# Half of the MLP weights' lower parts formed by an adding DMA instead of VectorE

## The chip, the cores and the metric

The kernel runs on one core of a Trainium2 chip. A core has five engines with queues of their own: TensorE (PE, matmuls; its weight loads are shown as PEld), VectorE (DVE), ScalarE (ACT), GpSimd (POOL) and SyncE (SP, which here only issues transfers). Sixteen DMA engines carry out the transfers that SP, ACT and POOL issue. SBUF is the on-chip memory with 128 partitions, PSUM holds the matmuls' sums.

The metric is the time of one execution in microseconds. The kernel before took 1623.62 us (median of two runs, 1623.09 to 1624.16).

## The reference

One layer of a decoder with 256 tokens behind 16 meta tokens and a width of 2048: a mixer (forgetting attention beside gated linear attention), then an MLP with squared ReLU and 8192 hidden channels. All is float32. What matters for the change is the MLP:

```python
def squared_relu_mlp(xn, w1, w2):
    return jnp.square(jax.nn.relu(xn @ w1)) @ w2

def reference(x, meta_tokens, ...):
    ...
    for l in range(DEPTH):
        h = h + hybrid_mixer(rmsnorm(h, norm_mix_g[l]), w_in[l], ...)
        h = h + squared_relu_mlp(rmsnorm(h, norm_mlp_g[l]), w_ff1[l], w_ff2[l])
    return rmsnorm(h, final_norm_g)[:, N_META:]
```

## The kernel before

**Numbers in two parts.** PE multiplies in a format (`F32R`) with fewer bits than float32. So every operand is split: an upper part `hi`, which is the value rounded to that format, and a lower part `lo`, which is the value less `hi`. A product of two split operands is made of three: `hi` times the upper and lower parts of the activations, and `lo` times their upper part. In `mac2` the first two are one matmul over 512 columns (line 136) and the third is one over 256 (line 137); both go to one PSUM bank `ps`.

**Weights in blocks.** The host lays all weights out as one array `w_all` of blocks of 2048 rows by 128 columns, in the order in which they are used (`stream`). A block is 128 partitions by 16 pieces (`KT`) of 128 columns, 1 MiB. It is fetched and split in two halves of eight pieces (`HK`), 512 KB each, by `weight_half`, whose `step` is:

```python
nc.sync.dma_start(raw[:, cols], w_all[c][:, i * HK * P + cols.start : i * HK * P + cols.stop])
r = raw.rearrange("p (k m) -> p k m", m=P)[:, k, :]
nc.scalar.copy(hi[:, k, :], r)
nc.vector.tensor_tensor(lo[:, k, :], r, hi[:, k, :].bitcast(F32), op=ALU.subtract)
```

So SP issues the load of `raw` (line 118), ACT rounds it to `whi` (line 120, a cast), and DVE subtracts to get `wlo` (line 121). `raw`, `whi` and `wlo` have five buffers each, for five halves, two and a half blocks. `next_weights` calls this for both halves of the next block; `gemm2` runs the 16 pairs of matmuls of a block.

**The MLP.** It goes through the hidden channels in four groups (`NG`). Each group has 16 blocks of the first matrix (ff1, lines 824 to 831), each followed by `relu2`, which evicts `ps`, applies the squared ReLU and splits the result to `a`; and then 16 blocks of the second matrix (ff2, lines 833 to 839), each followed by `add_residual`, which adds `ps` to the residual stream `ht`. In the last group the last four ff2 blocks (`NL`) are made in another way, with the upper parts of their weights kept (lines 842 to 875), since the final norm and the output are overlapped with them. In that group `square_sum` also adds up the squares for the final norm, on POOL (line 768). The output projection ahead of the MLP (lines 791 to 796) does the same for the MLP's norm.

**What sets the order.** The program is written block after block. A scheduler with a model of the times then sets the order of instructions on each engine, so that loads and splits run ahead of the matmuls as far as the buffers allow. Each engine works through its queue in order, and waits on semaphores for what it needs from others. A transfer issued by POOL stands in POOL's queue, with what POOL computes.

Of the kernel before, what the change touches and what calls it, by code (L numbers as in the profile page):

```python
# [7 lines left out]
F32 = mybir.dt.float32  # L8
# [3 lines left out]
AF = mybir.ActivationFunctionType  # L12
ALU = mybir.AluOpType
# [3 lines left out]
P = 128  # L17
# [48 lines left out]
def trunk(ctx: ExitStack, tc: tile.TileContext, hT, w_small, w_all, consts, w_alpha2, out):  # L66
    nc = tc.nc
    serial = [0]

    def nm(s):  # L70
        serial[0] += 1
        return f"{s}_{serial[0]}"
# [11 lines left out]
    def bank(pool, s):  # L84
        return pool.tile([P, 512], F32, tag="bank", name=nm(s))
# [7 lines left out]
    def issued():  # L93
        for e in list(waiting):
            e[0] -= 1
            if e[0] <= 0:
                waiting.remove(e)
                e[1]()
# [6 lines left out]
    chunk = [0]  # L105
    HK = KT // 2

    def weight_half(c, i, hi=None):

        raw = wp.tile([P, HK * P], F32, tag="raw", name=nm("raw"), bufs=RAW)  # L110
        if hi is None:
            hi = wp.tile([P, HK, P], F32R, tag="whi", name=nm("whi"))
        lo = wp.tile([P, HK, P], F32R, tag="wlo", name=nm("wlo"))

        def step(k0, n):
            k = slice(k0, k0 + n)
            cols = slice(k0 * P, (k0 + n) * P)
            nc.sync.dma_start(raw[:, cols], w_all[c][:, i * HK * P + cols.start : i * HK * P + cols.stop])
            r = raw.rearrange("p (k m) -> p k m", m=P)[:, k, :]
            nc.scalar.copy(hi[:, k, :], r)  # L120
            nc.vector.tensor_tensor(lo[:, k, :], r, hi[:, k, :].bitcast(F32), op=ALU.subtract)  # L121

        return hi, lo, step

    def next_weights(keep_hi=None):
        c = chunk[0]
        chunk[0] += 1
        parts = []
        for i in range(2):
            hi, lo, step = weight_half(c, i, None if keep_hi is None else keep_hi[:, HK * i : HK * (i + 1), :])  # L130
            step(0, HK)
            parts.append((hi, lo))
        return lambda k: (parts[k // HK][0][:, k % HK, :], parts[k // HK][1][:, k % HK, :])

    def mac2(ps, hi, lo, x, first, last):
        nc.tensor.matmul(ps, hi, x, start=first, stop=False)  # L136
        nc.tensor.matmul(ps[:, 0:NT], lo, x[:, 0, :], start=False, stop=last)  # L137

    def gemm2(w, x, k0=0, nk=KT):

        ps = bank(pg, "ps")
        for k in range(nk):
            hi, lo = w(k0 + k)
            mac2(ps, hi, lo, x[:, k], k == 0, k == nk - 1)
        issued()
        return ps

    def gemm_all(w, x, n=NA):

        ps = bank(pg, "psa")  # L150
        for k in range(KT):
            hi, lo = w(k)
            nc.tensor.matmul(ps[:, 0:n], hi, x[:, k, 0, :], start=(k == 0), stop=False)  # L153
            nc.tensor.matmul(ps[:, 0:n], lo, x[:, k, 0, :], start=False, stop=False)  # L154
            nc.tensor.matmul(ps[:, 0:n], hi, x[:, k, 1, :], start=False, stop=(k == KT - 1))  # L155
        issued()
        return ps
# [63 lines left out]
    def operand(pool, name, per_k, per_half, at=0, tag=None):  # L221


        kw = {} if tag is None else {"tag": tag}
        t = pool.tile([P, KT, per_k], F32R, name=nm(name), **kw)
        return t[:, :, at : at + per_half + NT].rearrange("p k (o t) -> p k o t", t=NT) if per_half == NT else \
            t[:, :, at : at + 2 * per_half].rearrange("p k (o t) -> p k o t", t=per_half)[:, :, :, 0:NT]
# [25 lines left out]
    def gain(i, k):  # L253
        return h[:, k, NA + i : NA + i + 1]
# [57 lines left out]
    for s in range(KT // 2):  # L312
# [5 lines left out]
        for kk in range(2):  # L318
            k = 2 * s + kk
# [41 lines left out]
    for i in range(2):  # L361
        hi = wp.tile([P, HK, P], F32R, tag="whi", name=nm("whi"))
        lo = wp.tile([P, HK, P], F32R, tag="wlo", name=nm("wlo"))
# [73 lines left out]
    def gla_gates(ts):  # L437
        sg = att.tile([P, 4, NT], F32, tag="sg", name=nm("sg"))
        for i in range(4):
            t = ts[i] if ts else total(gemm2(next_weights(), x[:, :, :, NM:NA]))  # L440
            nc.vector.tensor_tensor(t, t, rbt, op=ALU.mult)
            nc.scalar.activation(sg[:, i, :], t, AF.Sigmoid)
            nc.vector.tensor_tensor(sg[:, i, :], sg[:, i, :], t, op=ALU.mult)
        return sg
# [13 lines left out]
    def gla_head(hd, sg, ready=None):  # L458
# [4 lines left out]
        for i in range(2):  # L463
            ps = ready[1] if ready and i == 0 else gemm_all(next_weights(), x)
            nc.vector.tensor_tensor(ki[:, i, :], ps[:, 0:NA], rb, op=ALU.mult)
        for i in range(2):
            t = qd[:, i, :] if ready else total(gemm2(next_weights(), x[:, :, :, NM:NA]))
            nc.vector.scalar_tensor_tensor(qd[:, i, :], t, GLA_DK ** -0.5, rbt, op0=ALU.mult, op1=ALU.mult)
# [140 lines left out]
    ps = gemm_all(lambda k: (small[k // HK][0][:, k % HK, :], small[k // HK][1][:, k % HK, :]), x)  # L609
# [150 lines left out]
    x2 = operand(keep, "x2", 528, NT, tag="s2")  # L760

    def square_sum(j, acc):
        if j == 0:
            nc.scalar.activation(acc, ht[:, j, :], AF.Square)
        else:
            sq = gat.tile([P, NT], F32, tag="hsq", name=nm("hsq"))
            nc.scalar.activation(sq, ht[:, j, :], AF.Square)  # L767
            nc.gpsimd.tensor_tensor(acc, acc, sq, op=ALU.add)  # L768

    def add_residual(j, ps):  # L770
        b = tmp.tile([P, NT], F32, tag="evb", name=nm("evb"))
        nc.scalar.copy(b, ps[:, NT:512])
        nc.vector.tensor_tensor(ht[:, j, :], ps[:, 0:NT], ht[:, j, :], op=ALU.add)
        nc.vector.tensor_tensor(ht[:, j, :], ht[:, j, :], b, op=ALU.add)
# [38 lines left out]
    def relu2(a, f, ps):  # L813
        t = total(ps)
        nc.vector.scalar_tensor_tensor(t, t, 0.0, r2b, op0=ALU.max, op1=ALU.mult)
        s = gat.tile([P, NT], F32, tag="asq", name=nm("asq"))
        nc.vector.tensor_tensor(s, t, t, op=ALU.mult)
        split_to(a[:, f, 0, :], a[:, f, 1, :], s)

    acc = gat.tile([P, NT], F32, tag="acc", name="acc3", bufs=1)  # L820
    for g in range(NG):
        a = operand(keep, "a", 544, 272, tag="s1")
        held = []
        for f in range(KT):
            ps = gemm2(next_weights(), x2)
            if g == 0 and f == 0:
                held.append(ps)
                continue
            if g == 0 and f == 1:
                relu2(a, 0, held.pop())  # L830
            relu2(a, f, ps)
        last = g == NG - 1
        for j in range(KT - NL if last else KT):
            add_residual(j, gemm2(next_weights(), a))
            if last:
                square_sum(j, acc)
                nc.scalar.activation(ht[:, j, :], ht[:, j, :], AF.Identity, scale=gain(2, j))
                if j == 0:
                    tc.keep_in_program_order(nc.scalar.preload_act_table_set("sqrt_and_others"))
# [4 lines left out]
    for n in range(NL):  # L844
        j, ps = KT - NL + n, bank(pg if n < 3 else px, "ps")
# [49 lines left out]
    v, p, none = nc.vector, nc.gpsimd, lambda: None  # L895
# [81 lines left out]
```

## Time and profile before

| | |
|---|---|
| median of the runs | 1623.62 us |
| the profiled execution's own time | 1623.76 us |
| its span on the chip (first to last instruction) | 1621.7 us |
| granted TensorE clock, mean | 0.997 |
| DMA packets, data moved | 90841, 292.96 MB |
| mean rate | 181 GB/s |

How to read the profile: it shows one execution. An engine's busy time is the time in which it ran instructions, and for PE this is not PE at its peak, since matmuls are pipelined. A line number such as L121 is that of the code line that made the instruction. The chain of waits is followed back from the last instruction, at each step to what released it, or to the instruction before it on its engine. The DMA share is the mean share of the time in which the 16 DMA engines had a packet in work; it can pass 1, where packets overlap. "To landing" is from a transfer's issue to its completion. q1 is the queue of SP's transfers, q0 that of POOL's (software_dynamic).

The MLP fills the span from about 900 us on. In its steady part the rows of the 40 equal slices of the span read 9 of 10 for PE in all of them, and 5 of 10 for the DMA engines.

### The profile page before, as it was taken

The page shows a single profiled execution, that of the slowest core. Times are in us where ns is not written, and L with a number is a line of the kernel's source. Part 1 is how long each engine was busy: PE and PEld are TensorE (multiplying, and loading weights), DVE is VectorE, ACT ScalarE, POOL GpSimd, SP SyncE. Part 2 cuts the span into 40 slices and gives each one's busy share as a digit, 9 for nine tenths or more (in the row PEclk, how much of TensorE's full clock was granted, in tenths as well). Part 3 has the DMA queues.
Part 4 walks back from the last instruction along what each step waited for, and adds up shares of the span by engine and source line. Part 5 has one row for each costly group of instructions (what it writes and reads, how often), then busy time and mean ns, then how long its engine had stood idle before and what let it go on. Part 6 is the DMA issues. An engine that isn't in the chain of part 4 may idle for free.

```text
span 1621.7 us, 25628 instructions
## 1 busy us (share of the span) xinstructions
PE 1609.0 (99%) x10000; PEld 1447.0 (89%) x10000; DVE 1030.6 (64%) x1589; ACT 787.8 (49%) x1212; POOL 92.8 (6%) x144
## 2 busy tenths in 40 slices
PE   9999999999999999999999999999999999999997
PEld 8999999999998888888888888888888888888887
DVE  7866747476555555555677766567655676567654
ACT  6655444454445444444555444444444444444553
POOL 1000000010000000000011000000000000000022
PEclk9999999999999999999999999999999999999998
DMA  9444445454445555555555555555565555555552
GB/s 315 149 142 159 163 158 170 155 197 158 156 157 174 189 186 191 185 191 185 190 188 192 183 189 188 190 187 189 181 195 188 190 187 189 188 189 188 187 180 89
DMA packets 90841, 292.96 MB, mean 181 GB/s; under 512 B 9160, under 2 KB 21712, under 8 KB 90592
## 3 DMA queue, kind: packets, MB, share of 16 engines
q1 hardware_dynamic: 89472, 289.69, 55.1%
q8 instruction: 78, 1.28, 0.3%
q0 software_dynamic: 176, 1.12, 0.2%
q10 hardware_dynamic: 1072, 0.52, 0.1%
q14 instruction: 43, 0.35, 0.1%
HBM read 289.19 MB, written 2.11 MB: 180 GB/s over the span
## 4 chain that ended last, share of the span: by engine, by line
PE 99%; DMA 0%; ACT 0%; DVE 0%; SPq 0%; issue 0%; DVEq 0%; ACTq 0%
PE ps L136 51%; PE ps L137 26%; PE psa L155 5%; PE psa L154 5%; PE psa L153 5%; PE ps L334 1%; PE ps L864 1%; PE ps L339 1%; PE pa L504 1%; PE ps L848 0%; DMA h<-hT_dram 0%; PE po L568 0%; PE pz L402 0%; PE po L569 0%; PE pq L665 0%; PE po L182 0%
## 5 line engine op out<-in xcount | busy, mean ns | idle before, releaser
L121 DVE TENSOR_TENSOR wlo<-raw,whi 128x1024 fp32r<-128x1024 f32 x522 | 639.7, 1225 | 497.4 <-ACT whi L120 496.1
L120 ACT CAST whi<-raw 128x1024 fp32r<-128x1024 f32 x522 | 548.3, 1050 | 744.1 <-PE ps L136 502.0
L136 PE MATMUL ps<-x,whi 128*128 128x512 f32 x1952 | 685.8, 394 | 0.0
L137 PE MATMUL ps<-x,wlo 128*128 128x256 f32 x1952 | 548.0, 281 | 0.0
L136 PEld LDWEIGHTS ps<-x,whi 128*128 128x128 f32 x1952 | 366.4, 188 | 83.2
L137 PEld LDWEIGHTS ps<-x,wlo 128*128 128x128 f32 x1952 | 367.1, 188 | 0.0
L136 PE MATMUL ps<-a,whi 128*128 128x512 f32 x960 | 335.8, 394 | 0.0
L137 PE MATMUL ps<-a,wlo 128*128 128x256 f32 x960 | 269.7, 282 | 0.0
L136 PEld LDWEIGHTS ps<-a,whi 128*128 128x128 f32 x960 | 180.1, 188 | 41.0
L153 PE MATMUL psa<-x,whi 128*128 128x272 f32 x640 | 186.3, 291 | 0.0
L155 PE MATMUL psa<-x,whi 128*128 128x272 f32 x640 | 186.0, 291 | 0.0
L154 PE MATMUL psa<-x,wlo 128*128 128x272 f32 x640 | 184.5, 288 | 0.0
L137 PEld LDWEIGHTS ps<-a,wlo 128*128 128x128 f32 x960 | 181.4, 189 | 0.4
L153 PEld LDWEIGHTS psa<-x,whi 128*128 128x128 f32 x640 | 121.1, 189 | 0.7
L154 PEld LDWEIGHTS psa<-x,wlo 128*128 128x128 f32 x640 | 120.4, 188 | 0.2
L155 PEld LDWEIGHTS psa<-x,whi 128*128 128x128 f32 x640 | 120.2, 188 | 0.1
L136 PE MATMUL ps<-og,whi 128*128 128x512 f32 x256 | 89.9, 393 | 0.0
L136 PE MATMUL ps<-y,whi 128*128 128x512 f32 x256 | 89.1, 392 | 0.0
L768 POOL TENSOR_TENSOR acc<-acc,hsq 128x256 f32<-128x256 f32 x26 | 28.8, 1110 | 774.4 <-ACT hsq L767 774.4
L137 PE MATMUL ps<-y,wlo 128*128 128x256 f32 x256 | 71.8, 281 | 0.0
L137 PE MATMUL ps<-og,wlo 128*128 128x256 f32 x256 | 71.7, 280 | 0.0
L165 DVE TENSOR_TENSOR evt<-ps,evb 128x256 f32<-128x256 f32 x158 | 65.8, 417 | 0.2 <-ACT evb L162 0.2
(263 smaller groups left out, 1384.7 us busy)
## 6 DMA issues: line engine op xcount, KB each, us to landing
raw<-w_all_dram SPq DMA_DIRECT2D x537, 512.0 KB, 4.0
raw<-w_all_dram SPq DMA_DIRECT2D x7, 384.0 KB, 6.0
h<-hT_dram SPq DMA_DIRECT2D x7, 275.0 KB, 6.1
out_dram<-h SPq DMA_DIRECT2D x5, 256.0 KB, 2.6
negc<-fdram POOLq DMA_DIRECT2D x1, 1088.0 KB, 6.1
raw<-w_all_dram SPq DMA_DIRECT2D x2, 256.0 KB, 3.7
raw<-w_all_dram SPq DMA_DIRECT2D x2, 192.0 KB, 3.8
room<-w_small_dram SPq DMA_DIRECT2D x1, 320.0 KB, 6.9
```

The lines of the kernel that those rows point to most:

```text
L120: nc.scalar.copy(hi[:, k, :], r)
L121: nc.vector.tensor_tensor(lo[:, k, :], r, hi[:, k, :].bitcast(F32), op=ALU.subtract)
L136: nc.tensor.matmul(ps, hi, x, start=first, stop=False)
L137: nc.tensor.matmul(ps[:, 0:NT], lo, x[:, 0, :], start=False, stop=last)
L153: nc.tensor.matmul(ps[:, 0:n], hi, x[:, k, 0, :], start=(k == 0), stop=False)
L154: nc.tensor.matmul(ps[:, 0:n], lo, x[:, k, 0, :], start=False, stop=False)
L155: nc.tensor.matmul(ps[:, 0:n], hi, x[:, k, 1, :], start=False, stop=(k == KT - 1))
L165: nc.vector.tensor_tensor(t, ps[:, 0:NT], b, op=ALU.add)
L334: nc.tensor.matmul(ps, hi, x[:, k, :, NM:NA], start=st, stop=False)
L339: nc.tensor.matmul(ps[:, 0:NT], lo, x[:, k, 0, NM:NA], start=False, stop=sp)
L504: nc.tensor.matmul(dst, k[:, a, :], q[:, a, :], start=(a == 0), stop=(a == 1))
L768: nc.gpsimd.tensor_tensor(acc, acc, sq, op=ALU.add)
```

## The change

`weight_half` has a new argument, `by_dma`. Where it is set, DVE makes no subtraction. ACT writes the negated upper part into the lower part's buffer (line 123 of the new file), and POOL issues a transfer that reads the same 512 KB of weights from memory once more and adds them onto that buffer (line 124). `next_weights` sets it for the second half (`i == 1`) of a block only, and the MLP's two calls of `gemm2` ask for it. This holds for the 64 ff1 blocks and for 60 of the 64 ff2 blocks; the last four ff2 blocks, and all blocks ahead of the MLP, are split as before. Of these lines, the numbers shift by seven: the matmuls of `mac2` are lines 143 and 144 in the new file.

```diff
-    def weight_half(c, i, hi=None):
+    def weight_half(c, i, hi=None, by_dma=False):
...
             nc.scalar.copy(hi[:, k, :], r)
-            nc.vector.tensor_tensor(lo[:, k, :], r, hi[:, k, :].bitcast(F32), op=ALU.subtract)
+            if by_dma:
+                nc.scalar.activation(lo[:, k, :], hi[:, k, :].bitcast(F32), AF.Copy, scale=-1.0)
+                nc.gpsimd.dma_start(lo[:, k, :].rearrange("p k m -> p (k m)"),
+                                    w_all[c][:, i * HK * P + cols.start : i * HK * P + cols.stop], accum_op=ALU.add)
+            else:
+                nc.vector.tensor_tensor(lo[:, k, :], r, hi[:, k, :].bitcast(F32), op=ALU.subtract)
...
-    def next_weights(keep_hi=None):
+    def next_weights(keep_hi=None, by_dma=False):
...
-            hi, lo, step = weight_half(c, i, None if keep_hi is None else keep_hi[:, HK * i : HK * (i + 1), :])
+            hi, lo, step = weight_half(c, i, None if keep_hi is None else keep_hi[:, HK * i : HK * (i + 1), :],
+                                       by_dma and i == 1)
...
-            ps = gemm2(next_weights(), x2)
+            ps = gemm2(next_weights(by_dma=True), x2)
...
-            add_residual(j, gemm2(next_weights(), a))
+            add_residual(j, gemm2(next_weights(by_dma=True), a))
```

In the orders of instructions that the prediction quotes, `whi`, `wlo` and `raw` are the three tiles of a half, `evb` is an eviction, `a` and `asq` the activations between ff1 and ff2, `hsq` and `acc` a square and the sum of squares; the number behind a name tells one buffer's use from another's. DMASW in a wait stands for a transfer that POOL issued.

## The prediction

> **What bounds the kernel now.** I read the page first: busy time, then the chain that ended last.
>
> ```profile
> span 1621.7 us, 25628 instructions
> PE 1609.0 (99%) x10000; PEld 1447.0 (89%) x10000; DVE 1030.6 (64%) x1589; ACT 787.8 (49%) x1212; POOL 92.8 (6%) x144
> PE 99%; DMA 0%; ACT 0%; DVE 0%; SPq 0%; issue 0%; DVEq 0%; ACTq 0%
> ```
>
> PE is the chain. DVE, which the change relieves, is on it with 0%. Next come all the waits of PE in the whole run, and the stages: in each row the length, busy us of the five engines, the granted clock, the DMA engines' busy share and GB/s.
>
> ```profile
> PE pn L902 <- ACT d L901: 1.9, 1, 1.9
> PE ps L334 <- ACT whi L278: 1.3, 1, 1.3
> PE warm L307 <- DVE ones L188: 1.3, 1, 1.3
> PE pn L884 <- ACT sq L869: 0.8, 1, 0.8
> ...
> 10.00:20.00 10.00, 8.71 (x53) 7.56 (x52) 8.00 (x12) 8.94 (x13) 0.00 (x0) 1.00 1.09 361
> 1000.00:1500.00 500.00, 500.00 (x2862) 438.51 (x2862) 320.16 (x445) 224.80 (x313) 0.00 (x0) 1.00 0.58 189
> ```
>
> Four waits, 5.3 us together, none in the MLP; there (second stage row) PE is busy for all of 500 us at the full clock. So there is nothing to win in the MLP, and under 1% anywhere: 1621.7 - 1609.0 = 12.7 us. The first stage row is the fullest ten microseconds of the DMA engines: share 1.09 (packets overlap) at 361 GB/s. The MLP uses 0.58 of them. What the change adds lands on these engines, so the question is what is left there.
>
> Now the weights' path. From the page, the two halves of a split and the matmuls that use them; from the timeline of ACT, two blocks of the MLP (start, duration, operation, idle before); from the waits between 900 and 1500 us, what ACT and DVE wait for.
>
> ```profile
> L121 DVE TENSOR_TENSOR wlo<-raw,whi 128x1024 fp32r<-128x1024 f32 x522 | 639.7, 1225 | 497.4 <-ACT whi L120 496.1
> L120 ACT CAST whi<-raw 128x1024 fp32r<-128x1024 f32 x522 | 548.3, 1050 | 744.1 <-PE ps L136 502.0
> ...
> 1099.98 1.05 ACT L120 CAST whi<-raw 128x1024 fp32r<-128x1024 f32 x1 [1.48 <-issue]
> 1100.94 0.36 ACT L162 COPY evb<-ps 128x256 f32<-128x256 f32 x1
> 1102.73 1.05 ACT L120 CAST whi<-raw 128x1024 fp32r<-128x1024 f32 x1 [1.43 <-PE ps L136]
> 1103.69 0.40 ACT L169 CAST a<-asq 128x256 fp32r<-128x256 f32 x1
> 1105.57 1.05 ACT L120 CAST whi<-raw 128x1024 fp32r<-128x1024 f32 x1 [1.48 <-issue]
> ...
> ACT whi L120 <- PE ps L136: 236.5, 158, 1.8
> DVE wlo L121 <- ACT whi L120: 205.1, 205, 3.7
> ```
>
> One block takes 1105.57 - 1099.98 = 5.59 us, one half 2.795 us. ACT's cast waits for PE to free a buffer. There are five buffers for halves, so a half whose buffer comes free at T is multiplied from T + 4 x 2.795 = T + 11.18 us on. Everything that makes its upper and lower part has 11.18 us.
>
> Last the transfers: between 900 and 1500 us (queue with packets, MB and share; issues with KB and us to landing), in the fullest stretch 10 to 20, and around the one large transfer that POOL issues, 320 to 330.
>
> ```profile
> q1 hardware_dynamic: 30856, 112.33, 57.8%
> raw<-w_all_dram SPq DMA_DIRECT2D x215, 512.0 KB, 3.8
> ...
> DMA packets 3244, 3.61 MB, mean 361 GB/s; under 512 B 145, under 2 KB 2872, under 8 KB 3244
> ...
> q0 software_dynamic: 144, 1.11, 32.8%
> q1 hardware_dynamic: 305, 1.12, 27.6%
> negc<-fdram POOLq DMA_DIRECT2D x1, 1088.0 KB, 6.1
> ...
> L635 POOL DMA_DIRECT2D negc<-fdram x1: 607/607/607, 321.1 to 321.1; - x1
> ```
>
> The weight loads fill 57.8% of the engines: 0.578 x 5.59 = 3.23 us of every engine per block, 1.615 us per half, for 8 rows of 4 KB on each of 16 engines.
>
> **The change part by part.** It works on 64 ff1 blocks and 60 ff2 blocks (the last four keep the old form): 124 halves.
>
> DVE loses 124 x 1.225 = 152 us. By the rows above this is worth 0: DVE ends nothing that PE waits for.
>
> ACT gains 124 negations. No row shows one; the nearest is the cast of the same 128x1024 shape, 1.05 us, so 130 us. Per block ACT then has 3 x 1.05 + 0.36 + 0.40 = 3.91 of 5.59 us. On ACT, in the middle of ff1, a block was two casts of weights, one eviction (evb) and one cast of activations (a); before:
>
> ```order
> L120 CAST whi_10037<-raw_10036 128x1024
> L169 CAST a_9411<-asq_9918 128x256
> L120 CAST whi_10085<-raw_10084 128x1024
> L162 COPY evb_9967<-ps_9934 128x256
> L120 CAST whi_10091<-raw_10090 128x1024
> ```
>
> and after:
>
> ```order
> L121 CAST whi_9987<-raw_9986 128x1024
> L169 COPY evb_9867<-ps_9834 128x256
> L121 CAST whi_9993<-raw_9992 128x1024
> L123 ACTIVATE wlo_9994<-whi_9993 128x1024
> L176 CAST a_9411<-asq_9872 128x256
> ```
>
> The negation stands right behind its cast, and delays only the activations' cast, by about a microsecond; they are used in ff2. Value 0; if the cover went, 130 us.
>
> POOL issues 124 transfers (607 ns for one by L635: 75 us of an engine with nothing else there). On POOL, at the seam from the output projection to ff1, three of them stand among the additions of squares:
>
> ```order
> L775 TENSOR_TENSOR acc_8546<-acc_8546,hsq_9298 128x256
> L124 DMA wlo_9420<-w_all_dram 128x1024
> L775 TENSOR_TENSOR acc_8546<-acc_8546,hsq_9352 128x256
> L124 DMA wlo_9485<-w_all_dram 128x1024
> L775 TENSOR_TENSOR acc_8546<-acc_8546,hsq_9406 128x256
> L124 DMA wlo_9554<-w_all_dram 128x1024
> ```
>
> An addition of squares comes once a block, so one such queueing costs at most a block, 5.59 us, once; I take 0, as the five buffers cover it. SP's queue keeps its order.
>
> PE takes its second half's lower part from a transfer now, not from DVE. On PE, in the last ff2 group, second half of a block, after:
>
> ```order
> L143 MATMUL ps_15641<-a_14478,whi_15635 128x512 [waits Activation_49]
> L144 MATMUL ps_15641<-a_14478,wlo_15636 128x256 [waits DMASW7_49,Activation_49]
> L143 MATMUL ps_15641<-a_14478,whi_15635 128x512
> L144 MATMUL ps_15641<-a_14478,wlo_15636 128x256
> L143 MATMUL ps_15641<-a_14478,whi_15635 128x512
> ```
>
> PE is in order, so a late transfer stops all that follows. The time to spare: 11.18 less cast, negation and one small operation (1.05 + 1.05 + 0.40 = 2.5) leaves 8.7 us from issue to landing. The nearest rows are 3.8 us (512 KB from SP) and 6.1 us (1088 KB from POOL). So as long as the engines keep up, it is in time, by 2.6 us or more.
>
> That leaves the engines. The adding transfer reads 512 KB from memory again, reads the 512 KB of the negated part, and writes them. No row shows an adding transfer. Bounds: one plain transfer, 1.615 us (if the second read is free), and three (if it goes as one pass to fetch the old rows, one to add, one to write back). I take two, since its two reads for one write are twice the reads of the nearest row. That POOL issues it adds nothing: the 1088 KB of POOL's queue took 32.8% of 10 us x 16 engines for 1.11 MB, SP's at its side 27.6% for 1.12 MB.
>
> The Trainium skill, Collectives: The Full Stack, in its section on the bandwidth ceiling and fold count, says the same of reductions in flight: the add itself costs no cycles, but needs two source reads on one ring, which halves the rate. No trace here can show it; by that rule the cost would be two plain transfers as well.
>
> The engines' capacity for a block is 1.09 x 5.59 = 6.09 us, at the highest share seen.
>
> - one plain transfer: 3.23 + 1.615 = 4.85 us, it fits: 0;
> - two: 3.23 + 3.23 = 6.46 us, over by a factor of 1.06: a block takes 6.46 / 1.09 = 5.93 us, +0.34, and 124 x 0.34 = +42 us;
> - three: 8.08 / 1.09 = 7.41 us, +1.82, x 124 = +226 us.
>
> The sum: 0 (DVE) + 0 (ACT) + 0 (POOL) + 42 (DMA engines). The profiled execution took 1623.76 us (span 1621.7 and 2.1 around it; 0.1 above the median of the runs), so **1666 us**, with PE waiting for the adding transfers in the MLP. The bounds are 1624 and 1850.
>
> **The rivals.**
>
> *The transfer is hidden: 1624 us, no change.* The engines fit if an add costs up to (6.09 - 3.23) / 1.615 = 1.77 plain transfers, or if rows of 4 KB run faster than my price. For it: of the 3244 packets at 361 GB/s, 2872 were under 2 KB, and longer rows may do better; and between 320 and 330 SP's 1.12 MB, 273 rows of 4 KB, took 0.276 x 160 = 44.2 us of engine time, 0.162 us a row, so that a block with an add at two would need 32 x 0.162 = 5.2 us, under 5.59. Against it: at the MLP's own price, 3.23 / 16 = 0.202 us a row, it does not. The Trainium skill, DMA: Bandwidth & Descriptors, section Where 436 GB/s comes from, gives 435 GB/s as the ceiling; by it the 2 MiB of a block would take an estimated 4.8 us, and this rival would hold. The best ten microseconds here stay below, at 361.
>
> *The add costs more than three: above 1850 us.* Each row is read, added and written before the next, and the pass does not overlap; at four plain transfers a block takes 9.69 / 1.09 = 8.89 us, +3.30 x 124 = +409, 2033 us. Nothing in the trace speaks for or against it.
>
> *The landing comes too late though the engines have room.* It decides from 8.7 us after issue: at 9.7 us PE stands 1 us in every block, 1748 us. Against it are 3.8 and 6.1 us.
>
> *Faster.* It would need PE to wait in the MLP; it does not. That the change does not do what it says is out: its rows stand on ACT and POOL above.
>
> **How the numbers follow.** An add between 1.95 and 3 plain transfers, my forecast's case: 0.36, and 0.05 for 1.77 to 1.95, where the engines bind but the loss is within 2% (2% is 32 us, 0.26 us a block, 5.85 x 1.09 = 6.38 us, 1.95 transfers). Hidden: 0.38. Above three: 0.16. Late with room: 0.03. Faster: 0.02. The forecast's case, bound by the engines with 1.77 to 3, has 0.41 and is the likeliest by a little; its time is that of two, 1666. Range: from 1616, some us under no change, to the bound of three, 1850; outside are what lies above three and little else, 0.18. Within 2%, about what a measurement of this kernel can tell from no change: 0.38 + 0.05 = 0.43. Slower: 0.36 + 0.16 + 0.03 = 0.55. Faster by over 2%: 0.02.
>
> **What would show it.** Right: between 1000 and 1500 us PE under 95% busy, its waits on the matmul of the lower part with a DMA as releaser, the DMA share at 1 or above, POOL's queue with a share about as large as SP's for half its bytes, and the adding transfer's landing near or above 8.7 us. Wrong: PE at 500 of 500 us and a DMA share of 0.87 (one plain) to about 1 with no waits: hidden. A POOL queue with a share far over 0.58, or a share under 1 with PE waiting, would say that not the bytes but the add, or its latency, is the price. DVE must show 152 us less, ACT 130 us more; if PE waits for ACT instead, the cover of the negation failed.

## The result, and the profile after

The changed kernel took 1643.24 us (median of two runs, 1641.67 to 1644.82), 19.6 us more than before. The ratio is 1.0121, with a 95% interval of 1.0077 to 1.0165, so it is slower, but by less than the 2% that counted as slower in the prediction. The forecast was 42 us more.

The page of the changed kernel: its span, the busy engines, the chain that ended last.

```profile
span 1643.1 us, 26036 instructions
PE 1615.3 (98%) x10000; PEld 1448.8 (88%) x10000; DVE 884.5 (54%) x1465; ACT 914.9 (56%) x1336; POOL 195.0 (12%) x268
PE 80%; issue 13%; DMA 4%; POOL 2%; ACT 1%; DVE 0%; SPq 0%; POOLq 0%; DVEq 0%; ACTq 0%
```

The engines' loads moved as the change says: DVE has 146 us less, ACT 127 us more, POOL 102 us more. DMA and POOL now have 6% of the chain, where both had nothing. (The 13% "issue" is time along the followed chain for which the profile shows no wait; PE, at 98% of the span, did not stand still for it.) PE is busy for 6.3 us more than before and idle for 15.1 us more (27.8 of its span, 12.7 before).

All waits of PE in the changed kernel that are longer than one microsecond in total (total, times, longest), and two of its stages in the columns of the stage rows before:

```profile
PE ps L144 <- DMA wlo<-w_all_dram: 12.8, 11, 3.0
PE ps L341 <- ACT whi L285: 2.4, 2, 1.7
PE pn L909 <- ACT d L908: 1.9, 1, 1.9
PE warm L314 <- DVE ones L195: 1.3, 1, 1.3
PE ps L144 <- ACT a L176: 1.1, 1, 1.1
```

```profile
1000.00:1500.00 500.00, 494.75 (x2821) 432.11 (x2820) 210.17 (x347) 314.14 (x395) 76.83 (x88) 1.00 1.02 279
1560.00:1600.00 40.00, 35.63 (x193) 30.52 (x192) 14.48 (x20) 25.55 (x37) 8.40 (x10) 0.96 0.87 235
```

The new wait is the foretold one, PE for the adding transfer. But it came 11 times, not 124 times. The DMA share is 1.02, near the highest seen before (1.09), and PE still worked 494.75 of 500 us.

The transfers of the changed kernel between 900 and 1500 us (queue with packets, MB, share; issues with KB and median us to landing):

```profile
q0 software_dynamic: 15234, 55.49, 51.7%
q1 hardware_dynamic: 30468, 110.93, 49.7%
...
raw<-w_all_dram SPq DMA_DIRECT2D x212, 512.0 KB, 6.2
wlo<-w_all_dram POOLq DMA_DIRECT2D x105, 512.0 KB, 7.8
```

An add took 0.517 x 600 / 105 = 2.95 us of every engine, a load 0.497 x 600 / 212 = 1.41 us: 2.1 to 1. The add lands in 7.8 us, the loads in 6.2 where they took 3.8.

Where the time went shows best when the start of each block's first matmul is compared between the two traces. Of a lag of 21.7 us at the last matmul of the last four blocks, this came in each stage:

| ahead of the MLP | ff1, ff2 of group 1 | group 2 | group 3 | group 4: ff1, 12 blocks of ff2 | last four blocks |
|---|---|---|---|---|---|
| 0.7 | 1.3, 1.9 | 0.2, 3.3 | 0.0, 1.8 | 0.0, 12.1 | 0.4 |

In ff1 of groups 3 and 4 the lag does not grow at all, though each block has its add. The loss falls at the seams, above all a few blocks into ff2, and in the last group's ff2, in whose twelfth and last block with an add alone it grows by 3.6 us. The four blocks behind it, which have no adds, lose almost nothing. So it is not a price for each add.

One seam, in the changed kernel's timeline of ACT (start, duration, operation, idle before):

```profile
1350.55 1.05 ACT L121 CAST whi<-raw 128x1024 fp32r<-128x1024 f32 x1 [1.48 <-PE ps L143]
1351.63 1.06 ACT L123 ACTIVATE wlo<-whi 128x1024 fp32r<-128x1024 f32 x1
1352.60 0.39 ACT L176 CAST a<-asq 128x256 fp32r<-128x256 f32 x1
1355.80 1.05 ACT L121 CAST whi<-raw 128x1024 fp32r<-128x1024 f32 x1 [2.81 <-PE ps L143]
1357.44 1.06 ACT L121 CAST whi<-raw 128x1024 fp32r<-128x1024 f32 x1 [0.59 <-PE ps L143]
1358.39 0.37 ACT L779 COPY evb<-ps 128x256 f32<-128x256 f32 x1
1358.65 1.06 ACT L123 ACTIVATE wlo<-whi 128x1024 fp32r<-128x1024 f32 x1
```

then POOL's issues there:

```profile
1352.99 0.87 POOL L124 DMA_DIRECT2D wlo<-w_all_dram  x1 [4.71 <-ACT a L176]
1360.01 0.87 POOL L124 DMA_DIRECT2D wlo<-w_all_dram  x1 [6.16 <-ACT wlo L123]
1364.20 0.87 POOL L124 DMA_DIRECT2D wlo<-w_all_dram  x1 [3.31 <-ACT wlo L123]
```

and PE, when it gets on:

```profile
1369.41 0.39 PE L144 MATMUL ps<-a,wlo 128*128 128x256 f32 x1 [1.51 <-DMA wlo<-w_all_dram]
```

In the steady part casts come every 2.8 us and adds every 5.59. Here ACT waits 2.81 us for PE to free a buffer, the next negation stands behind a cast and an eviction, and the add goes out 7.02 us after the one before it, 1.43 us behind its turn. It lands 9.4 us after its issue, 1.6 later than the median, and PE stands for 1.51 us.

From this came three theories. **Theory A**, lateness: the engines keep up, and PE waits only where the order of the work leaves an add less time than it takes to land. **Theory B**, throughput, my prediction's: the engines are full, and each add pays. **Theory C**: the negation in ACT's queue, or the new order, costs the time, not the transfer.

### The profile page after: what moved, and what is told of

Read it like the earlier page. It is cut to its first block, busy times and chain, and to the rows that moved or that the text cites. A ratio compares the mean times of both kernels' runs of the same rounds, so it can differ in the third digit from the quotient of the medians.

```text
span 1643.1 us, 26036 instructions
## 1 busy us (share of the span) xinstructions
PE 1615.3 (98%) x10000; PEld 1448.8 (88%) x10000; DVE 884.5 (54%) x1465; ACT 914.9 (56%) x1336; POOL 195.0 (12%) x268
## 4 chain that ended last, share of the span: by engine, by line
PE 80%; issue 13%; DMA 4%; POOL 2%; ACT 1%; DVE 0%; SPq 0%; POOLq 0%; DVEq 0%; ACTq 0%
PE ps L143 38%; PE ps L144 20%; PE psa L162 5%; PE psa L161 5%; PE psa L160 5%; DMA wlo<-w_all_dram 3%; POOL wlo L124 2%; PE ps L341 1%; PE ps L871 1%; DMA raw<-w_all_dram 1%; PE ps L346 1%; PE pa L511 1%; PE ps L855 0%; DMA h<-hT_dram 0%; PE po L575 0%
## 5 line engine op out<-in xcount | busy, mean ns | idle before, releaser
L127 DVE TENSOR_TENSOR wlo<-raw,whi 128x1024 fp32r<-128x1024 f32 x398 | 487.9, 1226 | 545.6 <-ACT whi L121 544.4
L124 POOL DMA_DIRECT2D wlo<-w_all_dram x124 | 108.4, 875 | 554.4 <-ACT a L176 287.5
L123 ACT ACTIVATE wlo<-whi 128x1024 fp32r<-128x1024 f32 x124 | 131.3, 1059 | 3.4
L177 DVE TENSOR_TENSOR a<-asq,a 128x256 fp32r<-128x256 f32 x64 | 27.1, 425 | 104.5 <-ACT a L176 104.5
```

Of the source, the lines that this page charges most:

```text
L123: nc.scalar.activation(lo[:, k, :], hi[:, k, :].bitcast(F32), AF.Copy, scale=-1.0)
L124: nc.gpsimd.dma_start(lo[:, k, :].rearrange("p k m -> p (k m)"), w_all[c][:, i * HK * P + cols.start : i * HK * P + cols.stop], accum_op=A ...
L177: nc.vector.tensor_tensor(dst_lo, src, dst_hi.bitcast(F32), op=ALU.subtract)
```

## Experiments: buffers and places

**The last group's ff2 without adds.**

```diff
-            add_residual(j, gemm2(next_weights(by_dma=True), a))
+            add_residual(j, gemm2(next_weights(by_dma=not last), a))
```

> The 12 ff2 blocks of the last group take their second half from DVE again; 112 adds stay. Theory A (lateness: the DMA engines keep up, and time is lost only where the order of the work leaves an add less than the 7.8 us that it takes to land): the last group and the tail lost 11.8 of the 21.0 us between the two traces, so about 1631 us. Theory B (throughput: the engines are full, and every add pays its share): 12 of 124 adds less, about 2 us less, 1641 us.

Measured: 1630.96 us, ratio 1.0052 (1.0037 to 1.0067). Twelve adds of 124, a tenth, held 12.3 of the 19.6 us. As A had it, 1631; B's 1641 is out. (The expectation's 11.8 of 21.0 us is 12.5 of 21.7 by the table above, which moves A's figure by less than 1 us.)

**A sixth buffer in the MLP.**

```diff
+    def own(s):
+        return gat.tile([P, HK, P], F32R, tag="own" + s, name=nm(s), bufs=1)
...
-            hi = wp.tile([P, HK, P], F32R, tag="whi", name=nm("whi"))
-        lo = wp.tile([P, HK, P], F32R, tag="wlo", name=nm("wlo"))
+            hi = own("whi") if by_dma and c % 3 == 2 else wp.tile([P, HK, P], F32R, tag="whi", name=nm("whi"))
+        lo = own("wlo") if by_dma and c % 3 == 2 else wp.tile([P, HK, P], F32R, tag="wlo", name=nm("wlo"))
```

> In the MLP every third block's second half gets an upper and a lower buffer of its own, so six halves are buffered there instead of five; the adds and their bytes are the same. Theory A: an add has 2.8 us more until it is used, and of the stalls only the largest one (4.7 us, in the last group) is longer than that: 1625 to 1632 us. Theory B: the bytes are the same, 1640 to 1645 us.

Measured: 1631.01 us, ratio 1.0044 (1.0027 to 1.0061), with all 124 adds in place. So the same bytes cost 12 us less when they have more time. The stages say what it did: the last group's ff2 lost 1.2 us where it had lost 12.1, group 2's 0.0 where it had lost 3.3. But ff1 of the first group lost 4.4 instead of 1.3, near the MLP's start.

**Both together.**

> The own sixth buffer and the last group's ff2 on DVE together; 112 adds. Each alone took about 12 us off the loss of 20. Theory A: the two remove different stalls in part (the one the seams, the other the last group), so at most about 4 us stay: 1623 to 1628 us. If both merely cut one common cost, it stays near 1631 us.

Measured: 1628.65 us, ratio 1.0030 (1.0019 to 1.0041), 4.9 us over before and just above the expected range. Lost are 2.1 us at the MLP's start, 0.5 in ff2 of group 2 and 1.7 in ff2 of group 3; the sixth buffer did not take this last stall away in either run.

**Four buffers, and the control.** The edit is one number, once in the changed kernel and once in the kernel before. It takes a buffer from `whi` and `wlo`; `raw` keeps its five:

```diff
-    wp = ctx.enter_context(tc.tile_pool(name="wp", bufs=5))
+    wp = ctx.enter_context(tc.tile_pool(name="wp", bufs=4))
```

> Four buffers for the halves instead of five, in the whole program, with the adds. In ff1 an add is issued 2.44 us after its cast begins and takes 7.8 us to land, 10.2 us, where five buffers give 11.2 and four give 8.4. Theory A: now every block is late, the period grows until 1.5 blocks hold the 9 to 10.2 us: 6.1 to 6.8 us a block, 1690 to 1780 us. Theory B: buffers do not matter, 1640 to 1650 us.

> The control to it: the kernel before with four buffers. A half needs only the cast and the subtraction, some 2.6 us of 8.4, so theory A expects at most a few us of loss at the seams, 1624 to 1630 us; a large loss here would make the four-buffer run worthless as evidence.

Measured, in one run each: 1760.96 us with the adds, 1623.69 us without (the kernel before with five: 1623.75). The kernel before does not need the fifth buffer; with the adds its loss costs 118 us. The changed kernel with four buffers, between 1000 and 1500 us: the stage row, the issues, and PE's wait over the whole run.

```profile
1000.00:1500.00 500.00, 444.42 (x2378) 379.98 (x2377) 176.84 (x289) 257.08 (x329) 65.66 (x75) 0.95 0.89 235
```

```profile
wlo<-w_all_dram POOLq DMA_DIRECT2D x75, 512.0 KB, 8.7
```

```profile
PE ps L144 <- DMA wlo<-w_all_dram: 92.5, 47, 5.7
```

The engines are emptier than with five buffers (0.89 to 1.02) and PE waits seven times as long. The lag now grows in ff1 as well, in jumps: by 17.5 and 13.4 us between the second and the last ff1 block of groups 3 and 4, where five buffers lost nothing. This is lateness without full engines, and B does not make it. The granted clock fell to 0.95 in this stage, so a part of the loss is a slower PE: its 2378 matmuls took 0.187 us each, where those before took 500 / 2862 = 0.175, an estimated 29 us more of this stretch, beside 55.6 us in which it stood idle.

**The add in two pieces.**

```diff
-                nc.gpsimd.dma_start(lo[:, k, :].rearrange("p k m -> p (k m)"),
-                                    w_all[c][:, i * HK * P + cols.start : i * HK * P + cols.stop], accum_op=ALU.add)
+                for q in range(0, n, n // 2):
+                    at = i * HK * P + cols.start + q * P
+                    nc.gpsimd.dma_start(lo[:, k0 + q : k0 + q + n // 2, :].rearrange("p k m -> p (k m)"),
+                                        w_all[c][:, at : at + n // 2 * P], accum_op=ALU.add)
```

> Each add is issued as two of 256 KB, one behind the other; bytes the same, issues twice as many. Theory A (lateness): PE needs the second piece half a half later, 1.4 us, and the first lands sooner, so most stalls (0.2 to 1.9 us each) shrink: 1626 to 1636 us. Theory B (throughput): the bytes are the same and more packets of overhead come on top: 1643 us or more.

Measured: 1637.84 us, ratio 1.0093 (1.0076 to 1.0110), with single runs from 1634.75 to 1640.71. The median is under the change's, against B, but above A's range. A piece of half the size still took 6.6 us to land where the whole took 7.8, so splitting buys little time. The interval overlaps that of the change, and I draw nothing more from it.

## Experiments: what an add costs

**The transfer writes instead of adding.**

```diff
-                                    w_all[c][:, i * HK * P + cols.start : i * HK * P + cols.stop], accum_op=ALU.add)
+                                    w_all[c][:, i * HK * P + cols.start : i * HK * P + cols.stop])
```

> The transfer by POOL stays, with its bytes from memory, but writes instead of adding, so the lower part is wrong by the upper part; the negation stays too. Two reads are the add's price (my prediction's step): the transfer takes about 1.5 us of each engine instead of 2.95, lands in 5 to 6 us, and the loss nearly goes, 1624 to 1630 us. If the loss comes from the negation on ACT or from the new order of instructions (theory C), it stays at 1640 to 1645 us.

Measured: 1626.35 us, ratio 1.0018 (1.0009 to 1.0028). The negation on ACT, POOL's 124 issues and the second read of the weights are all there, and 17 of the 19.6 us are gone. So C is out as the main cause; it is the adding. Between the MLP's start and the last block with such a transfer no stage loses as much as 0.1 us, and PE waits for one of these transfers just once, for 2.1 us, in that last block. Queue, issue and stage in the run that writes:

```profile
q0 software_dynamic: 12908, 47.02, 30.1%
...
wlo<-w_all_dram POOLq DMA_DIRECT2D x89, 512.0 KB, 5.7
```

```profile
1000.00:1500.00 500.00, 500.00 (x2863) 438.57 (x2861) 215.56 (x357) 318.40 (x400) 47.18 (x89) 1.00 0.87 283
```

A plain transfer takes 0.301 x 500 / 89 = 1.69 us of each engine, and lands 2.1 us sooner than the add.

**Adds for both halves.**

```diff
-                                       by_dma and i == 1)
+                                       by_dma)
```

> Both halves of the 124 blocks are made by adds, 248 in all. This prices the add: with 2.82 us of each engine for a block's loads and 2.95 for one add, as the changed kernel's queues show, a block needs 8.7 us against 1.09 x 5.59, so 8.0 us a block, about 1920 us. If those 2.95 us are mostly waiting that overlaps (the engines have far more room than the shares say), it stays under 1750 us.

Measured: 1881.58 us in one run, between the two expected cases and nearer to that of full engines. Here every block pays alike: in the steady part each block's start falls 2.05 us further behind, so a block takes 5.59 + 2.05 = 7.64 us. The queues and the stage between 1000 and 1500 us:

```profile
q0 software_dynamic: 18824, 68.53, 68.8%
q1 hardware_dynamic: 18801, 68.45, 36.3%
```

```profile
1000.00:1500.00 500.00, 399.98 (x2080) 315.40 (x2080) 83.38 (x196) 298.15 (x358) 113.82 (x130) 0.99 1.05 275
```

Equal bytes in both queues, and 68.8 to 36.3: an add costs 1.9 loads. Two loads and two adds fill the 7.64 us, so a load is 7.64 / (2 + 2 x 1.9) = 1.32 us of a full engine, and an add 2.5 us. A block with one add then needs 2 x 1.32 + 2.5 = 5.1 us of its 5.59. It fits, which is why ff1 loses nothing. (This reckons that the ratio of busy times is that of the true prices, and that the engines are full at 7.64 us, as the landing of 13.9 us for an add suggests. Were they not, both prices would be lower, and a block with one add would fit all the better.)

**Plain transfers for both halves.** The two edits above together: four plain transfers a block, the sum that the prediction made without any add in it.

> Both halves of the 124 blocks get a plain transfer by POOL instead of an add (so the lower parts are wrong by the upper parts), four plain transfers of 512 KB a block with the loads. This is the sum on which my prediction stood, without the add. At the prediction's price, 1.615 us of each engine for a transfer and 1.09 of capacity, a block takes 5.93 us, 1666 us. At the price that the run with both halves added gives when full, about 1.33 us, the four take 5.3 of 5.59 us and are hidden: 1624 to 1635 us, no steady loss in ff1.

Measured: 1629.29 us, ratio 1.0043 (1.0026 to 1.0060).

```profile
1000.00:1500.00 500.00, 499.69 (x2858) 438.11 (x2857) 112.89 (x266) 405.22 (x491) 93.96 (x178) 1.00 1.05 375
...
q0 software_dynamic: 25593, 93.17, 56.6%
q1 hardware_dynamic: 25742, 93.74, 48.5%
...
wlo<-w_all_dram POOLq DMA_DIRECT2D x178, 512.0 KB, 6.7
```

The engines moved 375 GB/s, above the 361 of the stretch that I had taken for their limit, and PE worked 499.69 of 500 us. Four plain transfers fit in a block. The share is 1.05 here and 1.02 in the changed kernel, and the loss 5.7 us against 19.6: a share at this height is not by itself what costs the time. For equal bytes POOL's queue took 56.6 / 48.5 = 1.17 times the engine time of SP's. An add took 0.688 x 500 / 130 = 2.65 us in the run with adds for both halves, a plain transfer of the same queue 0.566 x 500 / 178 = 1.59 us here: 1.7 to 1, both at a share of 1.05. DVE has 113 of 500 us here, and PE is no faster for it.

**A lonelier add.**

```diff
-                                       by_dma and i == 1)
+                                       by_dma and i == 1 and c % 4 == 0)
```

> The add is used in every fourth block only, 31 adds, with the engines at about 0.68. This shows how long a nearly lone add takes to land. Theory A in its simple form (7.8 us is the add queueing among loads) expects 5 to 6 us to landing, as the plain transfer, and no loss, 1623 to 1626 us. If the add's landing is long by itself, it stays at 6.5 us or more; the loss is then still at most 31/124 of 20 us, 5 us.

Measured: 1623.56 us in one run (before: 1623.55). No loss, as expected, but the landing is not what the simple form of A had said:

```profile
wlo<-w_all_dram POOLq DMA_DIRECT2D x22, 512.0 KB, 7.2
```

Over this stage the share was 0.71, but the 22 adds did not meet such empty engines: between their issue and their landing it was 0.91 in the mean, and 0.87 for the transfers that only write, which landed in 5.7 us. What this shows is that three adds of four less take 0.6 us off the landing, 7.2 for 7.8. The plain transfers of the run above took 6.7 us at 1.05, so an add lands later than a plain transfer even where the engines are less busy. How much of its 7.2 us is queueing behind loads was not separated.

**DVE negates.**

```diff
-                nc.scalar.activation(lo[:, k, :], hi[:, k, :].bitcast(F32), AF.Copy, scale=-1.0)
+                nc.vector.tensor_scalar(lo[:, k, :], hi[:, k, :].bitcast(F32), -1.0, None, op0=ALU.mult)
```

> DVE negates instead of ACT; everything else stays. Theory A: the add is issued about as late as before, so most of the loss stays, 1636 to 1645 us. Theory C (the negation waits in ACT's in-order queue behind evictions and squares, which makes the add late at the seams and in the last group): the loss halves or more, 1624 to 1634 us.

Measured: 1641.58 us in one run. The loss stays with ACT relieved of its negations, so it does not rest on the negation's place in ACT's queue. (The stalls fell in part elsewhere: group 3's ff2 lost 4.1 us here, 1.8 with ACT negating.)

## What of the prediction held, and which step failed

- **PE is the bound, relief of DVE worth nothing:** right. DVE fell by 146 us, and no variant's median came out faster than before.
- **The negation on ACT costs nothing:** right, near enough. With the transfer writing instead of adding, all is there but the add, and the loss is 2.8 us, for the negation, POOL's issues and the second read together.
- **POOL's issues cost nothing:** right in effect; the size was off: 0.87 us for an add (0.53 for a plain transfer in the run that writes, 47.18 / 89), where I took 0.61. "That POOL issues it adds nothing" was a misreading: my own rows, 32.8% against 27.6% for nearly equal bytes, are 1.19 to 1, and the run with plain transfers for both halves has 1.17.
- **An add costs two plain transfers:** right against SP's loads, 1.9 in the run with the fullest engines and 2.1 in the changed kernel; 1.7 against a plain transfer of its own queue. The Trainium skill's rule on two source reads, which it states for ring collectives (Collectives: The Full Stack, on the bandwidth ceiling and fold count), agrees with the ratio to the loads. That the second read is the reason was not tested.
- **"two: 3.23 + 3.23 = 6.46 us, over by a factor of 1.06":** wrong, and this is the step that failed. I priced a load at 1.615 us from engines that were 58% busy. The same load took 1.41 us of them in the changed kernel, at a share of 1.02, and 1.32 us by the run with adds for both halves. I read the difference as waiting inside a packet's time that overlaps when more is queued; no run shows what it is. The sum is 5.1 us in 5.59, not 5.93, so the term "124 x 0.34 = +42 us" is zero: in ff1 of groups 3 and 4, with an add in every block, the lag grew by 0.0 us. My capacity of 1.09 had been right enough (1.05 in the fullest runs); the price was not. I had the better row in hand, 0.162 us a row of 4 KB between 320 and 330 us, which gives 5.2 us, and set it against this price as the hidden rival.
- **"as long as the engines keep up, it is in time, by 2.6 us or more":** wrong too, and the 19.6 us come from here. I set the 8.7 us against the landing of plain transfers, 3.8 and 6.1 us. The add took 7.8 us in the median and up to 10.6 between 900 and 1500 us, so 0.9 us was to spare. That was enough in the steady blocks and not at the seams and in the last group. At the seam shown, an issue 1.43 us late and a landing 1.6 us longer used it up. The rival "late though the engines have room", to which I gave 0.03, is the mechanism; I had seen it as all or nothing, a stall in every block, and it was eleven waits and some smaller gaps.
- **The signs:** three came: PE's waits on the lower part's matmul for a DMA, the DMA share above 1, and POOL's queue with about SP's share (51.7% and 49.7%). Two did not: PE was 99% busy between 1000 and 1500 us, not under 95%, and the add landed in 7.8 us, not 8.7.
- **The range** held the time by luck: the bounds were made for the price of an add, and the loss came from its landing. The chances did not favour the outcome: within 2% had 0.43, slower 0.55.

Not settled: what exactly makes the seams late. The trace shows the buffer freed late by PE and the add issued 1.43 us behind its turn. The next add follows it after 4.19 us instead of 5.59, and both land late (9.4 and 9.9 us), so it is not excluded that the engines are short of room there for a few microseconds. The order of PE's matmuls at the seam was not varied by itself, and the scheduler may order a kernel with other buffers in another way. Nor was it tried why the last group's ff2, with more work on ACT and POOL, loses most; that its adds are what loses there is shown, by taking them out.

## What to carry to other kernels

Price a transfer from a stretch in which the engines are full, not by the busy time of packets on half-idle engines: here a load's fell from 1.615 us at a share of 0.58 to 1.32 us when full. Ask of a new step in a prefetch chain two things apart, whether it fits the rate, and whether it fits the time from a buffer's release to its use; here the first held and the second did not. A time to spare of less than a microsecond held here in the steady state and broke at the seams. So look for the stage with the least of it, and try one buffer fewer, in the old kernel too, and one more: a loss that follows the buffers is one of time, not of rate.

## What the runs showed of the hardware

- An adding transfer of 512 KB onto SBUF took 7.2 us to land when only every fourth block had one (a share of 0.91 while it was on its way), and 7.8 us at 1.02. A plain one from the same queue took 5.7 us at 0.87 and 6.7 us at 1.05.
- It took 1.9 to 2.1 times the engine time of a plain load of the same bytes from SP's queue, and 1.7 times that of a plain transfer from POOL's.
- The sixteen engines moved 375 GB/s for 500 us in rows of 4 KB, while PE worked at full clock beside them.
- Half the bytes shortened an add's landing only from 7.8 to 6.6 us, with two of them issued one behind the other.
